# RWKV-7 recurrence in four products a chunk instead of five, its preparation in two threads instead of one

## The chip, the core and the metric

One core of a Trainium2 chip runs the whole program in one launch. Times are device microseconds (us) of that core. TensorE (PE) does matrix products and loads their weights through a queue of its own (PEld); VectorE (DVE) and ScalarE (ACT) do element work; GpSimd (POOL) does more of it; SyncE (SP) issues the DMAs. Each engine runs its own instructions in the order in which they stand, and waits on semaphores for the others.

## The reference

One inference step of a streaming encoder, one layer, on 512 prompt frames and 32 sample frames (544 columns). An input projection feeds three branches: Mamba-2 (SSD), gated linear attention (GLA) and RWKV-7. Gated output projections, cross attention over 256 memory tokens and a final norm follow. The change lies in the RWKV-7 branch, 16 heads of 64:

```
def step(S, inp):
    r_t, w_t, k_t, v_t, kk_t, a_t = inp
    s_kk = jnp.einsum('bhvk,bhk->bhv', S, kk_t)
    S_new = (S * w_t[:, :, None, :] - s_kk[..., None] * (kk_t * a_t)[:, :, None, :]
             + v_t[..., None] * k_t[:, :, None, :]).astype(S.dtype)
    return S_new, jnp.einsum('bhvk,bhk->bhv', S_new, r_t)
```

The output also has a bonus, the sum over a head of r, k and a weight, times v.

## The kernel before

**Layout.** Features lie on the 128 partitions, the 544 frames along the free axis. A weight block is 128 by 1024; it is loaded (`wraw`), split into a high part (`wh`, ACT) and a low part (`wl`, DVE), and multiplied in 24 products of 272 columns for each half of the frames: the "dense" products, `pd`. There are 7584 of them, and 56 blocks (`fill`) are not needed early; their results go through two `fg` buffers on ACT to DRAM.

**The order.** A planner (`Sched`) writes one static order for each engine. Each piece of work is a generator (a thread) with a priority; when a thread waits for data the next one gets a turn, and `dense` (priority 9) puts five `pd` products at a time into TensorE's queue. The planner estimates each instruction's time (`Sched.mm` for products) and uses only these estimates to choose the order. DMAs are queued on SP when the planner thinks that their data are there.

**RWKV in the planner.** Heads are taken in pairs (p = 0 to 7), one head on partitions 0 to 63, one on 64 to 127, frames in nine chunks of 64 (eight of the prompt and one, padded, of the sample). For each pair: `rw_A` prepares (shift, decay `EE`, keys, the operands `ar` and `bk`), then makes the pairwise products `pp` within chunks, masks them into `NK`, stores the matrices to be inverted (`n_scr`), computes the bonus (`pbn`), and turns v and the scaled keys into token rows (`ptk`, `tm`, twelve `NK<-tm` DMAs and four `NK<-t`). It does all of it for pair p before it begins pair p + 1. `rw_I` inverts the 32 by 32 diagonal blocks on POOL in 62 instructions (`im`, `td`) after the DMAs `nd` and `td<-in_eye`; `rw_J` brings the result back through DRAM (`d_scr`, `TT`), transposes it on DVE, and makes the last block with products `pW` and `pT`. `rw_C` is the recurrence: `pr` for all chunks, then for each chunk one after the other the products `pc`. `rw_N` normalises and writes out. Pairs use three slots of buffers.

In a chunk with a state `Sn` (128 partitions by 64: head 0 above head 1) before, the five products are two with the state, one with the inverse `TT`, and two with `NK`:

```
S.mm(pa[:, 0:64], AR[:, c, 0:2, :].rearrange("p a t -> p (a t)"), Ss, True, True)
S.mm(px, AR[:, c, 2:4, :].rearrange("p a t -> p (a t)"), Ss, True, True)
S.tt(R, pa[:, 0:64], NK[:, c, 0, 0, :], ADD)
S.mm(pu, TTt[:, c, :], R, True, True)
nc.vector.copy_predicated(VU, two(C("blk1").bitcast(I32)), both(pu))
    S.mm(pb[:, i * 64:i * 64 + 64], NK[:, c, i, 1:3, :].rearrange("p a t -> p (a t)"), VU[:, i, :], True, True)
```

All of these are full fp32 products, and the trace has two records for each. The recurrence has 72 chunks: 64 have a state before them, and the first prompt chunk of each of the eight pairs has none (one product with `TT` and two with `NK`).

Of the kernel before, what the change touches and what calls it, by code (L numbers as in the profile page):

```python
# [20 lines left out]
T = NP_ + NS  # L21
# [48 lines left out]
for _n, _c in (("ident", 128), ("blk1", 128), ("m_rw", 128), ("s65", 585), ("m_ssd", 128), ("s64", TP), ("s128", T)):  # L70
    CC.add(_n, _c)


def constants():
    c = np.zeros((128, CC.n), np.float32)

    def put(name, a):
        o, n = CC.at[name]
        c[:, o:o + n] = a

    p = np.arange(128)
    same = (p[:, None] // 64 == p[None, :] // 64).astype(np.float32)
    put("ident", np.eye(128))
    put("blk1", same)
    s = (p % 64)[:, None]
    t = np.arange(64)[None, :]
    put("m_rw", np.concatenate([s < t, s <= t], 1))
# [38 lines left out]
class Sched:  # L126
# [110 lines left out]
    def mm(self, out, lhsT, rhs, start, stop, transpose=False, shared=False):  # L237
# [102 lines left out]
def body(tc, I, O):  # L340
# [19 lines left out]
    with tc.manual_schedule(), \  # L360
# [418 lines left out]
        def make_slot(pool, i):  # L779

            d = dict(AR=pool.tile([128, 9, 4, 64], F32, name=f"AR{i}"))
# [10 lines left out]
        for i in range(2):  # L792
            nc.gpsimd.memset(f32(w2l[64 - 64 * i:128 - 64 * i, i]), 0.0)
        b_scr = dr.tile([8, 128, T], F32, name="b_scr")
# [83 lines left out]
        def rw_A(p):  # L878

            rs, ks, vs = (zt[p % 2][n_] for n_ in ("rs", "ks", "vs"))  # L880
            yield has("wa_s")
# [3 lines left out]
            if p < NSLOT:  # L885

                for h in (0, 64):
                    g = 64 - h
                    for x in (d["AR"][h:h + 64, :, 1:3, :] if h == 0 else d["AR"][h:h + 64, :, 0:4:3, :], d["TT"][h:h + 64, :, g:g + 64]):
                        nc.gpsimd.memset(x, 0.0)  # L890
                        S.note("p", 700, (x,), ())
# [29 lines left out]
            rn = rwp.tile([128, TP], F32, name="rn", tag="rn")  # L921
# [54 lines left out]
            for i in range(2):  # L976
                hs = slice(64 * i, 64 * i + 64)
                S.tt(ar[hs, :, 3 - i, :], ch(rs)[hs], EE[hs, :, 1:65], MUL)
# [18 lines left out]
            def tokens(n_, src):  # L997
# [8 lines left out]
                for i in range(2):  # L1006
                    h = 64 * i
                    g = h if n_ == 2 else 64 - h
                    for r in range(2):
                        S.store(out=nk[g:g + 64, r:8:2, i, 1 + i if n_ else 3, :], in_=tm[r * 64:r * 64 + 64, :, h:h + 64])  # L1010
# [5 lines left out]
            for c0, cn in ((0, 4), (4, 4), (8, 1)):  # L1016
# [3 lines left out]
                for c in range(cn):  # L1020
                    for i in range(2):
                        hs = slice(64 * i, 64 * i + 64)
                        S.mm(ps[i][:, c * 128:c * 128 + 128], bk[hs, c0 + c, i:i + 2, :].rearrange("p a t -> p (a t)"),
                             ar[hs, c0 + c, i:4 - i:3 - 2 * i], True, True)
                for i in range(2):
                    S.tt(nk[:, c0:c0 + cn, i, 0:3 - i:2 - i, :], ps[i][:, :cn * 128].rearrange("p (c a t) -> p c a t", c=cn, a=2),
                         two(C("m_rw")).unsqueeze(1).to_broadcast([128, cn, 2, 64]), MUL)
                yield S.free("v")
            for i in range(2):
                S.store(out=rows64(n_scr[p % 2], i), in_=nk[i * 64:i * 64 + 64, :, i, 0, :])  # L1030
            done.add(f"rwN{p}")

            r2 = rwp.tile([128, 3, TP], F32R, name="r2", tag="bk")
# [18 lines left out]
            for i in range(2):  # L1052
                h = 64 * i
                S.store(out=nk[64 - h:128 - h, 8, i, 1 + i:4:2 - i, :], in_=t8[:, 0:2, h:h + 64])
                S.store(out=nk[h:h + 64, 8, i, 1 + i, :], in_=t8[:, 2, h:h + 64])
# [37 lines left out]
        def rw_J(p):  # L1093
# [33 lines left out]

        def both(a):
# [3 lines left out]
        def rw_C(p):  # L1132
# [3 lines left out]
            s0r = rwp.tile([128, 64], F32, name="s0r", tag="s0r")  # L1136
            S.dma(out=s0r, in_=I["s0_rwkv"][:, p])
# [4 lines left out]
            yield S.at(s0r, NK, TTt)  # L1142
            for c0, cn in ((4, 5), (0, 4)):
                ps = yield from bank("pr")
                for c in range(cn):
                    for i in range(2):
                        hs, gs = slice(64 * i, 64 * i + 64), slice(64 - 64 * i, 128 - 64 * i)
                        S.mm(ps[hs, c * 64:c * 64 + 64], NK[gs, c0 + c, i, 0, :], NK[gs, c0 + c, i, 3, :], True, True)
                S.act(NK[:, c0:c0 + cn, 0, 0, :], ps[:, :cn * 64].rearrange("p (c t) -> p c t", t=64), AF.Copy)
            for c in [8] + list(range(8)):  # L1150
                Ss = s0r if c == 8 else (None if c == 0 else st_)
# [4 lines left out]
                pu, px = pa[:, 64:128], pb[:, 128:192]  # L1156
                VU, R = NK[:, c, :, 3, :], NK[:, c, 0, 0, :]
# [5 lines left out]
                yield S.at(R)  # L1163
                S.mm(pu, TTt[:, c, :], R, True, True)
                nc.vector.copy_predicated(VU, two(C("blk1").bitcast(I32)), both(pu))
                S.note("v", 203, (VU,), (pu,))
                yield S.at(VU)
                for i in range(2):
                    S.mm(pb[:, i * 64:i * 64 + 64], NK[:, c, i, 1:3, :].rearrange("p a t -> p (a t)"), VU[:, i, :], True, True)
                ns = rwp.tile([128, 64], F32, name="Sn", tag="S", bufs=2)  # L1170
                for i in range(2):
                    hs = slice(64 * i, 64 * i + 64)
                    if Ss is None:
                        S.cp(ns[hs], pb[hs, hs])
                    else:
                        S.stt(ns[hs], Ss[hs], GC[hs, c, :], pb[hs, hs], MUL, ADD)
                if c >= 7:
                    S.store(out=O["rwkv_s" if c == 8 else "rwkv_p"][:, p], in_=ns)
                st_ = ns
                yield S.at(ns)  # L1180
                for i in range(2):
                    gs = slice(64 - 64 * i, 128 - 64 * i)
                    S.act(NK[gs, c, 0, 3, :], pb[gs, i * 64:i * 64 + 64], AF.Copy)
                if Ss is not None:
                    S.act(NK[:, c, 1, 3, :], px, AF.Copy)
            done.add(f"rwC{p}")

        def rw_N(p):
# [4 lines left out]
            x = NK[:, :, 0, 3, :]  # L1193
            yield S.at(x)
# [7 lines left out]
            S.tt(x[:, 1:9], x[:, 1:9], NK[:, 1:9, 1, 3, :], ADD)  # L1202
            yield S.free("v")
            cs = rwr.tile([128, 9, 64], F32, name="cs", tag="cs")
            sq = rwr.tile([128, 9, 64], F32, name="sq2", tag="hi")
            S.stt(cs, sums("mean", x).to_broadcast([128, 9, 64]), -1.0 / 64, x, MUL, ADD)
# [753 lines left out]
        S.add(rw_all(rw_N, "rwN_end"), 2)  # L1960
        S.add(rw_all(rw_A), 3)
# [134 lines left out]
```

## Time and profile before

| what | value |
| --- | --- |
| median of 3 runs | 1306.12 us (1303.98 to 1306.37) |
| the profiled execution | 1309.07 us, of which its span 1307.3 us |
| PE busy | 1270.0 us, 97% of the span |
| DVE, ACT, POOL busy | 825.6, 637.2, 387.3 us |
| stretch with the recurrence | 165 to 665 us of the span |

The profile is of one execution. Its own time is 2.95 us above the median and 1.8 us above its span. Busy time of PE is from the start of a record to its modelled end, and records overlap, so the price of a product is read here from the distance between starts. A wait in the middle of a busy stretch shows only where it is longer than that overlap.

### The profile page before, as it was taken

How to read it: one execution, taken by the hardware profiler on the slowest of the kernel's cores; microseconds unless marked ns; L12 is line 12 of the kernel's file. 1: busy time of each engine (PE TensorE's matmuls, PEld its weight loads, DVE VectorE, ACT ScalarE, POOL GpSimd, SP SyncE). 2: the span in 40 equal slices, each digit the busy share in tenths (PEclk: the TensorE clock that was granted, in tenths of full speed). 3: DMA queues.
4: the chain of work that ended last, by engine and by line, in shares of the span. 5: the costliest groups of instructions: out<-in, count | busy, mean ns of one | idle time of the engine just before them, and what ended most of it. 6: DMA issues, size and time to landing. Idle time of an engine off the chain costs nothing.

```text
span 1307.3 us, 27775 instructions
## 1 busy us (share of the span) xinstructions
PE 1270.0 (97%) x10976; PEld 1226.2 (94%) x10976; DVE 825.6 (63%) x1643; ACT 637.2 (49%) x1263; POOL 387.3 (30%) x716
## 2 busy tenths in 40 slices
PE   8899998999999999999999999999999999999997
PEld 7899988999999999999999999988899999999997
DVE  5748646766766676754346687886666756575543
ACT  5664525375655555553455545463445423544422
POOL 0711747482827272833001062422300000000000
PEclk9999998999999999999999999998999999999999
DMA  8543544535353625364343243343698446540302
GB/s 290 161 140 92 148 100 130 132 118 134 121 127 111 153 90 148 122 161 134 109 168 122 91 127 109 115 132 104 231 337 288 140 136 189 170 146 25 105 17 70
DMA packets 170003, 181.10 MB, mean 139 GB/s; under 512 B 100096, under 2 KB 122720, under 8 KB 169744
## 3 DMA queue, kind: packets, MB, share of 16 engines
q1 hardware_dynamic: 169440, 178.64, 44.8%
q8 instruction: 87, 1.43, 0.5%
q10 hardware_dynamic: 432, 0.67, 0.2%
q14 instruction: 44, 0.36, 0.1%
HBM read 136.24 MB, written 35.39 MB: 131 GB/s over the span
## 4 chain that ended last, share of the span: by engine, by line
PE 81%; DVE 7%; ACT 3%; DMA 3%; POOL 3%; issue 2%; SPq 1%; POOLq 0%; ACTq 0%; DVEq 0%
PE pd L245 62%; PE pc L245 5%; PE pp L245 1%; DMA wraw<-in_wall 1%; DVE wl L284 1%; PE psc L245 1%; SPq L327 1%; PE pov L245 1%; PE pO L245 1%; PE py L245 1%; PE ptk L242 1%; DVE ul L293 1%; POOL im L284 1%; PE pl L245 1%; PE ph L245 1%
## 5 line engine op out<-in xcount | busy, mean ns | idle before, releaser
L245 PE MATMUL pd<-ul,wh 128*128 128x272 f32 (+1 forms) x1632 | 436.0, 295 | 0.0
L245 PE MATMUL pd<-uh,wh 128*128 128x272 f32 (+1 forms) x1632 | 432.5, 295 | 0.5 <-ACT wh L278 0.4
L245 PEld LDWEIGHTS pd<-ul,wh 128*128 128x128 f32 (+1 forms) x1632 | 309.1, 189 | 4.1 <-issue 2.4
L245 PEld LDWEIGHTS pd<-uh,wh 128*128 128x128 f32 (+1 forms) x1632 | 308.5, 189 | 4.0 <-ACT wh L278 1.6
L245 PE MATMUL pd<-uh,wl 128*128 128x272 f32 (+1 forms) x1632 | 252.5, 293 | 1.3 <-DVE wl L284 1.3
L245 PEld LDWEIGHTS pd<-uh,wl 128*128 128x128 f32 (+1 forms) x1632 | 221.1, 189 | 4.6 <-issue 1.9
L284 DVE TENSOR_TENSOR wl<-wraw,wh 128x1024 fp32r<-128x1024 f32 (+1 forms) x143 | 180.2, 1263 | 22.7 <-ACT wh L278 22.2
L278 ACT ACTIVATE wh<-wraw 128x1024 fp32r<-128x1024 f32 (+1 forms) x143 | 149.3, 1046 | 55.0 <-PE pd L245 36.4
L284 POOL TENSOR_TENSOR im<-td,nd 108x84 f32<-108x84 f32 (+23 forms) x248 | 106.0, 428 | 195.3 <-DMA td<-in_eye 86.2
L245 PE MATMUL pd<-uh,wr 128*128 128x256 f32 (+1 forms) x768 | 148.6, 291 | 1.4 <-ACT uh L278 1.4
L245 PEld LDWEIGHTS pd<-uh,wr 128*128 128x128 f32 x768 | 121.0, 188 | 3.0 <-ACT uh L278 1.6
L284 POOL TENSOR_TENSOR td<-td,im 108x84 f32<-108x84 f32 (+23 forms) x248 | 111.5, 450 | 19.4
L284 POOL TENSOR_TENSOR macc<-macc,hrs 128x288 f32<-128x288 f32 x3 | 2.3, 792 | 367.9 <-DVE macc L293 367.9
L245 PE MATMUL pd<-ul,wr 128*128 128x256 f32 (+1 forms) x384 | 100.2, 292 | 0.1
L245 PEld LDWEIGHTS pd<-ul,wr 128*128 128x128 f32 x384 | 72.4, 189 | 1.0 <-issue 0.4
L278 ACT ACT_TABLE_LOAD x55 | 70.6, 1283 | 2.6 <-DVE tB L284 1.6
L278 ACT ACTIVATE fg<-pd 128x272 f32<-128x272 f32 x64 | 25.1, 394 | 84.0 <-PE pd L245 62.6
L293 DVE SCALAR_TENSOR_TENSOR fg<-fg,pd 128x272 f32<-128x272 f32 x48 | 20.8, 435 | 61.6 <-ACT fg L278 61.4
L278 ACT ACTIVATE lerpA<-pd,par 128x272 f32<-128x272 f32 x50 | 24.3, 487 | 65.8 <-PE pd L245 61.1
L278 ACT ACTIVATE NK<-pc 64x64 f32<-64x64 f32 (+1 forms) x208 | 38.3, 214 | 34.2 <-DVE Sn L293 31.0
L278 ACT ACTIVATE fg<-pd,dpar 128x272 f32<-128x272 f32 x48 | 23.1, 484 | 61.1 <-PE pd L245 48.6
L293 DVE SCALAR_TENSOR_TENSOR Sn<-Sn,GC,pc 64x64 f32<-64x64 f32 x112 | 31.2, 279 | 25.7 <-PE pc L245 22.0
(470 smaller groups left out, 2479.5 us busy)
## 6 DMA issues: line engine op xcount, KB each, us to landing
wraw<-in_wall SPq DMA_DIRECT2D x165, 512.0 KB
g_mg<-fg SPq DMA_DIRECT2D x24, 272.0 KB
mgt<-g_mg SPq DMA_DIRECT2D x24, 272.0 KB
NK<-tm SPq DMA_DIRECT2D x96, 64.0 KB
ab<-acs_d SPq DMA_DIRECT2D x8, 512.0 KB
nd<-n_scr SPq DMA_DIRECT2D x24, 144.0 KB
n_scr<-NK SPq DMA_DIRECT2D x16, 144.0 KB
TT<-d_scr SPq DMA_DIRECT2D x16, 144.0 KB
```

The costliest lines, as they stand in the source:

```text
L242: self.nc.tensor.transpose(out, lhsT, rhs)
L245: self.nc.tensor.matmul(out, lhsT, rhs, start=start, stop=stop, skip_group_check=shared)
L278: self.nc.scalar.activation(out=out, in_=in_, func=f, scale=scale, bias=bias)
L284: eng.tensor_tensor(out=out, in0=a, in1=b, op=op)
L293: self.nc.vector.scalar_tensor_tensor(out=out, in0=a, scalar=s, in1=b, op0=op0, op1=op1)
L327: getattr(self.nc, q).dma_start(out=out, in_=in_)
```

## The change

**In `rw_C`** the state is held as a 128 by 128 block-diagonal tile `Sb` (three of them, zeroed once), so one product of 128 moving columns replaces the two with the state, and the product with `TT` gets 128 columns too. `R` is twice as wide. The three evacuations on ACT become two of 128 by 128. The state's load and its two stores become two DMAs of half the size each. For a chunk without a state POOL zeroes the place of the missing part (8 new instructions). `AR` halves, so 6 memsets of it go from POOL. **In `rw_N`** one addition over 128 partitions becomes two over 64. **The planner's estimate** for an fp32 product of over 64 rows out changes. **`rw_A` is cut** after the keys; the new thread `rw_B` has the rest. `rw_A(p+1)` may begin when `rw_A(p)` has ended; it waits for the bonus of pair p before it reuses `r2`, for the masked products before it reuses `bk`, and for `rwA{p-2}`.

```
-                ns = max(107.0, n * 1.67)
+                ns = max(220.0, n * 1.79)
...
+        Sb = [rwp.tile([128, 2, 64], F32, name=f"Sb{i}") for i in range(3)]
...
-            yield has("wa_s")
+            yield has("wa_s", *([f"rwA{p - 2}"] if p > 1 else []))
...
-            sq = rwp.tile([128, TP], F32, name="sq", tag="sq")
+            sq = rwp.tile([128, TP], F32, name="sq", tag="sq", bufs=2)
...
-            k2 = rwp.tile([128, 3, TP], F32R, name="k2", tag="bk")
+            if p:
+                yield has(f"rwB{p - 1}")
+            k2 = rwp.tile([128, 2, TP], F32R, name="k2", tag="r2")
...
+            if p:
+                yield has(f"rwN{p - 1}")
             bk = rwp.tile([128, 9, 3, 64], F32, name="bk", tag="bk")
...
+            hand[p] = rs, vs, kae, bee, bk, d
             done.add(f"rwK{p}")
-            yield has("rwR", f"vs{p}")
+        def rw_B(p):
+            yield has(f"rwK{p}", "rwR", f"vs{p}")
+            rk, vs, kae, bee, bk, d = hand.pop(p)
...
                 if Ss is not None:
-                    S.mm(pa[:, 0:64], AR[:, c, 0:2, :].rearrange("p a t -> p (a t)"), Ss, True, True)
-                    S.mm(px, AR[:, c, 2:4, :].rearrange("p a t -> p (a t)"), Ss, True, True)
-                    R = rwp.tile([128, 64], F32, name="R", tag="R")
-                    S.tt(R, pa[:, 0:64], NK[:, c, 0, 0, :], ADD)
+                    S.mm(pa[:, 0:128], AR[:, c].rearrange("p a t -> p (a t)"), Ss, True, True)
+                    r_ = rwp.tile([128, 2, 64], F32, name="R", tag="R")
+                    S.tt(r_, two(pa[:, 0:128]), R, ADD)
+                    R = r_
...
-                for i in range(2):
-                    gs = slice(64 - 64 * i, 128 - 64 * i)
-                    S.act(NK[gs, c, 0, 3, :], pb[gs, i * 64:i * 64 + 64], AF.Copy)
+                S.act(NB[:, c, 3:8:4, :], two(pb[:, 0:128]), AF.Copy)
                 if Ss is not None:
-                    S.act(NK[:, c, 1, 3, :], px, AF.Copy)
+                    S.act(NB[:, c, 0:7:6, :], two(pa[:, 0:128]), AF.Copy)
+                else:
+                    nc.gpsimd.memset(NB[:, c, 0:7:6, :], 0.0)
...
+        S.add(rw_all(rw_B), 3)
         S.add(rw_all(rw_A), 3)
```

Three places of the order show what moves. On TensorE, one step of the recurrence of pair 0, before:

```order
L245 MATMUL pc<-Sn,AR_119 128x64 x2
L245 MATMUL pd<-ul,wh 128x272
L245 MATMUL pd<-uh,wh 128x272
L245 MATMUL pd<-ul,wh 128x272
L245 MATMUL pd<-uh,wh 128x272
L245 MATMUL pd<-ul,wh 128x272
L245 MATMUL pc<-R,TT_121 128x64
L245 MATMUL pbn<-r_3026,blk_97 128x272 x4
L242 MATMUL ptk<-con,rn 128x128 x4
L245 MATMUL pc<-NK_120 128x64 x2
```

and the step of the same pair that stands first in the order of the change (`Sb` is the state, `R` the sum that goes into the product with `TT`):

```order
L245 MATMUL pc<-Sb_133,AR_119 128x128
L245 MATMUL pd<-ul,wh 128x272
L245 MATMUL pd<-uh,wl 128x272 x4
L245 MATMUL pc<-R,TT_121 128x128
L245 MATMUL pd<-uh,wl 128x272 x4
L245 MATMUL pd<-uh,wh 128x272
L245 MATMUL pd<-ul,wh 128x272
L245 MATMUL pd<-uh,wh 128x272
L245 MATMUL pd<-ul,wh 128x272
L245 MATMUL pd<-uh,wh 128x272
L245 MATMUL pc<-NK_120 128x64 x2
```

The two products of 128x64 with the state have become one of 128x128, the one with `TT` is 128x128, the two with `NK` are as they were, and five dense products stand between state and `TT` in both.

On ScalarE, the last rows before the evacuation of `pr` with which the recurrence of pair 0 begins, before:

```order
L278 ACTIVATE fg<-pd 128x272 x2
L278 ACTIVATE wh<-wraw 128x1024
L278 ACTIVATE W<-pW 128x256
L278 ACTIVATE TT_121<-pT 32x8x32 x2
L278 ACTIVATE fg<-pd 128x272
L278 ACTIVATE NK_120<-pr 128x5x64
L278 ACTIVATE NK_120<-pr 128x4x64
```

and now:

```order
L278 ACTIVATE fg<-pd 128x272
L278 ACTIVATE wh<-wraw 128x1024
L278 ACTIVATE lerpA<-pd,par 128x272
L278 ACTIVATE W<-pW 128x256
L278 ACTIVATE lerpA<-pd,par 128x272
L278 ACTIVATE wh<-wraw 128x1024
L278 ACTIVATE TT_121<-pT 32x8x32 x2
L278 ACTIVATE NK_120<-pr 128x5x64
L278 ACTIVATE NK_120<-pr 128x4x64
```

Of three `fg` evacuations ahead of `NK<-pr` one is left; `lerpA` (the token shift of later pairs) stands there instead.

On SP, from the store of the matrices of pair 1 (`n_scr`) to the load of its unit matrices (`td<-in_eye`), with which its inversion can begin; `d_scr` and `TT` belong to pair 0. Before:

```order
L327 DMA n_scr_135<-NK_124 64x9x64 x2
L327 DMA nd<-n_scr_135 36x32x32 x3
L327 DMA b_scr<-rs_109 128x544
L327 DMA NK_124<-tm 64x4x64 x8
L327 DMA td<-in_eye 108x352
L327 DMA g_rwkv<-fg 128x544
L327 DMA wraw<-in_wall 128x1024
```

and now:

```order
L327 DMA n_scr_141<-NK_124 64x9x64 x2
L327 DMA w2r<-in_w2a 128x256
L327 DMA b_scr<-rs_109 128x544
L327 DMA NK_124<-tm 64x4x64 x8
L327 DMA d_scr<-td 36x11x32
L327 DMA d_scr<-td 36x10x32
L327 DMA d_scr<-td 36x11x32
L327 DMA TT_121<-d_scr 64x9x64 x2
L327 DMA nd<-n_scr_141 36x32x32 x3
L327 DMA wraw<-in_wall 128x1024
L327 DMA td<-in_eye 108x352
```

The result of pair 0 (`d_scr`, `TT`) stood ahead of this piece; now it stands inside it, so the inversion of pair 1 follows directly on that of pair 0. Between the products `pW` of pair 0 and those of pair 1 TensorE has 312 dense products and 40 products `pc` before, 211 and 27 now; between pair 1 and pair 2 it has 297 and 39 before, 240 and 31 now. In all, TensorE's order has 64 products fewer; every other kind of product keeps its count.

## Rows read from the trace of the kernel before

**Rows 1.** The page: span, busy time of each engine, chain that ended last.

```profile
span 1307.3 us, 27775 instructions
PE 1270.0 (97%) x10976; PEld 1226.2 (94%) x10976; DVE 825.6 (63%) x1643; ACT 637.2 (49%) x1263; POOL 387.3 (30%) x716
PE 81%; DVE 7%; ACT 3%; DMA 3%; POOL 3%; issue 2%; SPq 1%; POOLq 0%; ACTq 0%; DVEq 0%
```

**Rows 2.** Windows, 165 to 665 us: length, busy us of each engine, clock, DMA share.

```profile
165.00:665.00 500.00, 489.59 (x4758) 475.06 (x4759) 305.98 (x667) 255.94 (x584) 239.93 (x517) 0.99 0.46 125
```

**Rows 3.** Waits of TensorE: us in total, times, longest.

```profile
PE pc L245 <- DVE R L284: 4.7, 2, 4.4
```

**Rows 4.** Timeline of a recurrence step of pair 7: start us, us, instruction.

```profile
653.35 0.65 PE L245 MATMUL pd<-uh,wl 128*128 128x272 f32 x4
653.84 0.55 PE L245 MATMUL pc<-Sn,AR 128*128 128x64 f32 x4
654.20 0.75 PE L245 MATMUL pd<-uh,wl 128*128 128x272 f32 x4
654.21 0.23 DVE L284 TENSOR_TENSOR R<-pc,NK 128x64 f32<-128x64 f32 x1 [0.89 <-PE pc L245]
654.79 0.33 PE L245 MATMUL pc<-R,TT 128*128 128x64 f32 x2
```

**Rows 5.** Timeline of fp32 products with 128 moving columns (GLA stage).

```profile
740.43 0.38 PE L245 MATMUL pO<-AT,vt 128*128 128x128 f32 x2
740.65 0.39 PE L245 MATMUL pO<-g_qe,gS 128*128 128x128 f32 x2
```

**Rows 6.** Tile `pc`: products with the state, ns min/median/max, first and last start.

```profile
L245 PE MATMUL pc<-Sn,AR x224: 217/275/323, 213.0 to 657.6; 128*128 128x64 f32 x112
L245 PE MATMUL pc<-s0r,AR x32: 275/275/323, 190.9 to 628.1; 128*128 128x64 f32 x32
```

**Rows 7.** Groups by form on DVE and ACT: count, busy us, mean ns, idle before.

```profile
L284 DVE TENSOR_TENSOR R<-pc,NK 128x64 f32<-128x64 f32 x64 | 14.2, 222 | 30.0 <-PE pc L245 20.9 <-ACT NK L278 5.2 <-PE pd L245 3.1
L284 DVE TENSOR_TENSOR NK<-pp,con 128x128 f32<-128x128 f32 x16 | 3.9, 285 | 0.7 <-PE pp L245 0.5
L278 ACT ACTIVATE NK<-pc 64x64 f32<-64x64 f32 x144 | 31.3, 218 | 34.2 <-DVE Sn L293 31.0 <-DVE Sn L305 1.2
L278 ACT ACTIVATE btok<-pcb 128x128 f32<-128x128 f32 x8 | 1.9, 264 | 4.0 <-PE pcb L245 3.9
```

**Rows 8.** Timeline, 185 to 201 us, of PE, SP and ACT.

```profile
185.85 0.83 PE L245 MATMUL pW<-x,NK 32*64 32x32 f32 x22
...
189.38 6.14 SPq L327 DMA_DIRECT2D NK<-tm  x8
...
196.24 0.35 SPq L327 DMA_DIRECT2D g_rwkv<-fg  x1
...
199.16 0.40 ACT L278 ACTIVATE fg<-pd 128x272 f32<-128x272 f32 x1 [9.94 <-DMA g_rwkv<-fg]
```

**Rows 9.** Windows right after that wait; columns as in rows 2.

```profile
200.20:206.20 6.00, 5.98 (x27) 5.98 (x28) 2.56 (x7) 3.58 (x7) 3.76 (x11) 0.51 0.72 262
```

**Rows 10.** Timeline of the inversion of pair 1 and the start of pair 2's.

```profile
198.54 0.24 POOL L284 TENSOR_TENSOR im<-td,nd 108x31 f32<-108x31 f32 x1 [19.75 <-DMA td<-in_eye]
...
239.94 1.28 SPq L327 DMA_DIRECT2D d_scr<-td  x3
...
244.01 1.28 SPq L327 DMA_DIRECT2D TT<-d_scr  x2
...
250.15 2.12 SPq L327 DMA_DIRECT2D nd<-n_scr  x3
...
252.16 1.12 PE L245 MATMUL pW<-x,NK 32*64 32x32 f32 x32
252.31 1.00 SPq L327 DMA_DIRECT2D td<-in_eye  x1
...
256.99 0.24 POOL L284 TENSOR_TENSOR im<-td,nd 108x31 f32<-108x31 f32 x1 [17.08 <-DMA td<-in_eye]
```

More of the change, by code (lines that the diff above doesn't have):

```diff
@@ L69 @@
 CC = Cols()
-for _n, _c in (("ident", 128), ("blk1", 128), ("m_rw", 128), ("s65", 585), ("m_ssd", 128), ("s64", TP), ("s128", T)):
+for _n, _c in (("ident", 128), ("blk1", 128), ("m_rw", 192), ("s65", 585), ("m_ssd", 128), ("s64", TP), ("s128", T)):
     CC.add(_n, _c)
@@ L86, in constants @@
     t = np.arange(64)[None, :]
-    put("m_rw", np.concatenate([s < t, s <= t], 1))
+    put("m_rw", np.concatenate([s < t, s <= t, s < t], 1))
     put("m_ssd", p[:, None] <= p[None, :])
@@ L793, in body @@
             nc.gpsimd.memset(f32(w2l[64 - 64 * i:128 - 64 * i, i]), 0.0)
+        Sb = [rwp.tile([128, 2, 64], F32, name=f"Sb{i}") for i in range(3)]
+        for t_ in Sb:
+            nc.gpsimd.memset(t_, 0.0)
         b_scr = dr.tile([8, 128, T], F32, name="b_scr")
@@ L888, in rw_A @@
                     g = 64 - h
-                    for x in (d["AR"][h:h + 64, :, 1:3, :] if h == 0 else d["AR"][h:h + 64, :, 0:4:3, :], d["TT"][h:h + 64, :, g:g + 64]):
-                        nc.gpsimd.memset(x, 0.0)
-                        S.note("p", 700, (x,), ())
+                    x = d["TT"][h:h + 64, :, g:g + 64]
+                    nc.gpsimd.memset(x, 0.0)
+                    S.note("p", 700, (x,), ())
             w2h = rwp.tile([128, 2, 128], F32R, name="w2h", tag="w2h")
@@ L1009, in tokens @@
                     for r in range(2):
-                        S.store(out=nk[g:g + 64, r:8:2, i, 1 + i if n_ else 3, :], in_=tm[r * 64:r * 64 + 64, :, h:h + 64])
+                        S.store(out=nk[g:g + 64, r:8:2, i, 1 if n_ else 3, :], in_=tm[r * 64:r * 64 + 64, :, h:h + 64])
                 yield S.free("a")
@@ L1023, in rw_A @@
                         S.mm(ps[i][:, c * 128:c * 128 + 128], bk[hs, c0 + c, i:i + 2, :].rearrange("p a t -> p (a t)"),
-                             ar[hs, c0 + c, i:4 - i:3 - 2 * i], True, True)
+                             ar[hs, c0 + c], True, True)
                 for i in range(2):
-                    S.tt(nk[:, c0:c0 + cn, i, 0:3 - i:2 - i, :], ps[i][:, :cn * 128].rearrange("p (c a t) -> p c a t", c=cn, a=2),
-                         two(C("m_rw")).unsqueeze(1).to_broadcast([128, cn, 2, 64]), MUL)
+                    S.tt(nk[:, c0:c0 + cn, i, 0:3:2, :], ps[i][:, :cn * 128].rearrange("p (c a t) -> p c a t", c=cn, a=2),
+                         two(C("m_rw")[:, 64 * i:64 * i + 128]).unsqueeze(1).to_broadcast([128, cn, 2, 64]), MUL)
                 yield S.free("v")
             for i in range(2):
-                S.store(out=rows64(n_scr[p % 2], i), in_=nk[i * 64:i * 64 + 64, :, i, 0, :])
+                S.store(out=rows64(n_scr[p % 2], i), in_=nk[i * 64:i * 64 + 64, :, i, 2 * i, :])
             done.add(f"rwN{p}")
-            r2 = rwp.tile([128, 3, TP], F32R, name="r2", tag="bk")
+            r2 = rwp.tile([128, 2, TP], F32R, name="r2", tag="r2")
             rh, rl = r2[:, 0], r2[:, 1]
@@ L1053, in rw_A @@
                 h = 64 * i
-                S.store(out=nk[64 - h:128 - h, 8, i, 1 + i:4:2 - i, :], in_=t8[:, 0:2, h:h + 64])
-                S.store(out=nk[h:h + 64, 8, i, 1 + i, :], in_=t8[:, 2, h:h + 64])
+                S.store(out=nk[64 - h:128 - h, 8, i, 1:4:2, :], in_=t8[:, 0:2, h:h + 64])
+                S.store(out=nk[h:h + 64, 8, i, 1, :], in_=t8[:, 2, h:h + 64])
             done.add(f"rwA{p}")
@@ L1135, in rw_C @@
             yield has(f"rwA{p}")
-            s0r = rwp.tile([128, 64], F32, name="s0r", tag="s0r")
-            S.dma(out=s0r, in_=I["s0_rwkv"][:, p])
+            for i in range(2):
+                S.dma(out=Sb[2][64 * i:64 * i + 64, i], in_=I["s0_rwkv"][64 * i:64 * i + 64, p])
             yield has(f"rwI{p}")
@@ L1141, in rw_C @@
             yield S.stored(NK)
[L1142 removed]
+            yield S.at(Sb[2], NK, TTt)
             for c0, cn in ((4, 5), (0, 4)):
@@ L1200, in sums @@
                 return t
-            S.tt(x[:, 1:9], x[:, 1:9], NK[:, 1:9, 1, 3, :], ADD)
+            for i in range(2):
+                gs = slice(64 - 64 * i, 128 - 64 * i)
+                S.tt(cs[gs], NB[gs, :, 6 * i, :], NB[gs, :, 3 + 4 * i, :], ADD)
             yield S.free("v")
-            cs = rwr.tile([128, 9, 64], F32, name="cs", tag="cs")
-            sq = rwr.tile([128, 9, 64], F32, name="sq2", tag="hi")
-            S.stt(cs, sums("mean", x).to_broadcast([128, 9, 64]), -1.0 / 64, x, MUL, ADD)
+            S.stt(cs, sums("mean", cs).to_broadcast([128, 9, 64]), -1.0 / 64, cs, MUL, ADD)
             done.add(f"rwO{p}")
```

44 lines of the change are left out of this document (26 added, 18 removed).

## The prediction

> **What bounds the kernel now.** First the busy shares and the chain that ended last [rows 1]: TensorE is busy for 97% of the span, and 81% of the chain is its own work. So the time is TensorE's work plus its waits, and a shorter chain on another engine is worth only the wait that it removes. Second the windows: in the stretch with the recurrence TensorE is busy for 489.6 of 500 us, while DVE, ACT and POOL have 306, 256 and 240 us of work [rows 2]; nothing else is near its limit there. The recurrence is a long chain, but dense products stand between its steps. If the chain gets shorter, these dense products are done later, beside the SSD and GLA stages; they are not saved. Third the waits: the longest of TensorE in that stretch is 4.4 us of the 4.7 us on the sum `R` [rows 3].
>
> **The products that go.** A fp32 product has two records. The price is the delay that it makes for the dense products behind it. Before the step of pair 7 four dense products take 0.49 us from start to start (653.35 to 653.84). The two products with the state start at 653.84, the next dense product at 654.20, 0.36 us later, and its four take 0.59 us, 0.10 us too many. So the two cost 0.46 us, 0.23 us each [rows 4]. Products with 128 moving columns start 0.22 us apart [rows 5]. So a product costs the same at 64 columns and at 128, to 0.01 us, and making the two remaining ones twice as wide is free, while one of five goes. The state's products of before are (224 + 32) / 2 = 128 [rows 6]; 64 are left. I take the lower price: 64 x 0.22 = 14.1 us less (14.7 us by the higher one).
>
> The Trainium skill says otherwise: "TensorE: Matmul & The Clock Gate", section "Back-to-back issue gap", lets the distance of matmuls grow with the moved columns. The rows just cited speak against it for these fp32 products; what it would make of the time stands with the rivals.
>
> **What the wider step costs elsewhere.** `R` goes from 128x64, 222 ns, to 128x128, for which the masked products have the same operation, shape and operands (PSUM and SBUF): 285 ns [rows 7]. That is 63 ns more between the state product and the one with `TT`. On ACT two evacuations of 128x128 at 264 ns, as `btok` shows, take the place of three smaller ones of which two are 218 ns [rows 7]; about 0.1 us less per chunk, on an engine that has time to spare. The addition in `rw_N` is one more DVE instruction in a pair, and its readers wait in a thread of their own: hidden by dense work, and without that cover less than 1 us a pair (the 128x128 sum takes 0.29 us, a quarter of the columns and twice the rows). The 24 more DMAs on SP, at 0.35 us as the store in rows 8, are 8.4 us of a queue that serves 500 us; I cost them at nothing, and if they fall into one of SP's piles they are part of the bound for SP below. The eight memsets on POOL wait for the product of a chunk that TensorE has reached by then; behind them stands the inversion of the next pair, which is where their cost would show.
>
> In the shown step `R` starts 0.37 us after the state product, takes 0.23, and TensorE reads it at 654.79, 0.35 us after its end. Between state and `TT` stand four or five dense products, about 0.6 us, at some 20 places before and now. The first state product was followed by a second of 0.22 us, which was cover; it is gone. At the tight places 0.22 + 0.06 us of cover is lost against the 0.35 us that the row shows to spare, so many should still fit. Bounds: nothing, or 64 x 0.063 = 4.0 us when every longer `R` is waited for. I take 2 us.
>
> The cut between `rw_A` and `rw_B` adds no instruction: its waits hold back the planner's threads, not an engine, and what they do is seen in the order alone. It brings the keys and products of the next pairs forward, which is where the next two points come from.
>
> **A wait that should go.** Until 200.2 us TensorE stands for 4.4 us for the first `R` of pair 0 [rows 3]. The chain behind it is in rows 8: SP is busy with eight `NK<-tm` from 189.38 for 6.1 us, the store `g_rwkv` gets its turn at 196.24, ACT's next `fg` waited 9.9 us for that store (both buffers full), and behind `fg` on ACT stand the evacuations that `R` needs. Right after it TensorE's clock is at 0.51, the lower of its two levels (1.2 of 2.4 GHz), for 6.0 us [rows 9]; that costs another 6.0 x 0.49 = 2.9 us. In the new order only one `fg` stands near there, and none between `W` and `NK<-pr`. So this wait should go: 7.3 us less. SP's pile is still there, longer by `d_scr`, `TT` and `nd`, so the same can happen to a weight load; then the gain is 0.
>
> **A wait that should come.** The inversions of the pairs now follow each other directly. One cycle, from one `TT` to the next, by rows 10: `TT` 1.3, `nd` 2.1, one weight load 0.4, `td` 1.0, from its end to the first POOL instruction 3.7, the 62 instructions 41.4 (198.54 to 239.94), then 4.1 from `d_scr` to `TT`, of which 2.6 us went to four `NK<-tm` ahead of it. (The weight load is put at about the 0.35 us of the store in rows 8.) That is 54 us at most. In pair 1 the order of before has eight other POOL instructions among the 62 (memsets, decays, keys), the new one two; 41.4 us over 70 is 0.6 us each, so some 3.5 us go, 38 stay, and without the `NK<-tm` the cycle is 48 us. So: 48 to 54. TensorE's own work between `pW` of pair 0 and of pair 1: before 252.16 - 185.85 = 66.3 us [rows 8, 10], less the 7.3 us above, 59.0; 101 dense products fewer at 0.123 and 13 `pc` fewer at 0.22 make it 43.7 us. Between pairs 1 and 2 it is about 47 us by the same counts. What is missing is 4 to 10 us at pair 1 and 1 to 7 at pair 2, less what lay between the landing of `TT` and `pW` (8.2 us from issue to `pW` in pair 1, of which the way through DRAM and the transposes need a part, perhaps half). From pair 3 on 269 to 293 dense products stand between, with room. I take 3 us at each of the two: 6 us. Bounds: 0, and 13 us.
>
> **The sum.** 1309.07 - 14.1 - 7.3 + 2 + 6 = 1295.7 us for an execution like the profiled one. That one was 2.95 us above the median of its three runs, so the median to expect is 1292.7: **1293 us**.
>
> **The rivals.**
>
> *The new waits give little or nothing back.* The inversion keeps up, and the longer `R` is hidden. 1306.1 - 14.1 - 7.3 = 1285 us. For it: POOL has half its time free in the stretch [rows 2]. Against: its work is one chain with DMAs at both ends.
>
> *The inversion becomes the pace (slower).* Place: `pW` of each pair, for `TT`. With 54 us a cycle pairs 1 and 2 miss 10 and 7 us, less 4: 13 us; two waits of such length would each bring a stretch at the lower clock as in rows 9, 5.8 us; with R's 2 us, -14.1 - 7.3 + 13 + 5.8 + 2 leaves 1305.5, no change. Some 53 to 55 us a cycle is the point that decides. At 58 us pairs 1, 2 and 4 miss 14, 11 and 6, less 4: 27 us and three slow stretches, 8.7: 1306.1 - 21.4 + 27 + 8.7 + 2 = 1322 us. For it: POOL's 41.4 us are of a stretch with fewer instructions on DVE per us. Against: six instructions fewer stand there in pair 1.
>
> *A wait is only moved.* The products go, but SP's pile holds up a weight load or an `fg` elsewhere at the old price: 1306.1 - 14.1 + 2 + 6 = 1300 us.
>
> *The columns set the price.* If a wide product cost 0.22 and a narrow one half of it, a chunk would cost 5 x 0.11 = 0.55 before and 2 x 0.22 + 2 x 0.11 = 0.66 now; 64 x 0.11 = 7 us more, 1313 us. This is the rule named above. Against it stands 0.23 against 0.22 in rows 4 and 5.
>
> *The change doesn't do what it says:* the order shows the 64 products gone, so only their price is open.
>
> **How the numbers follow.** Forecast as summed, 1288 to 1299: 0.50. Nothing given back, below 1288: 0.17. A wait only moved, 1299 to 1303.5: 0.12. Inversion near its deciding point, no change: 0.08; slower: 0.10. Columns: 0.03, slower. A measurement of this kernel tells apart about 0.2%, 2.6 us. So faster 0.79, same 0.08, slower 0.13. The range leaves a few in a hundred below (both gains and small waits of TensorE gone too) and the inversion's bad end above: 1282 to 1306.
>
> **What would show it.** Tile `pc` with 128 records for the state instead of 256, starts of a wide product still 0.22 us apart; no `fg` wait of 9.9 us; in TensorE's waits `pW` (through the DVE transpose or ACT) with a few us at pairs 1 and 2; POOL's 62 instructions of pair 1 in about 38 us. The prediction is wrong if TensorE's idle time in the stretch grows by over 14 us, or if the wide product costs more than 0.3 us.

## The result, and the profile after

The changed kernel takes **1316.84 us** (median of 4 runs, 1313.06 to 1320.48), the kernel before 1305.43 us in the same session: a ratio of 1.008 [1.006, 1.0099], slower by 0.8%. The forecast was 1293 us, range 1282 to 1306, with 0.13 for slower: outside the range, and of the wrong sign.

The page of the changed kernel: span, busy times, and the chain that ended last.

```profile
span 1318.6 us, 27544 instructions
PE 1270.8 (96%) x10848; PEld 1222.5 (93%) x10848; DVE 838.5 (64%) x1651; ACT 626.8 (48%) x1191; POOL 380.3 (29%) x721
PE 66%; DVE 8%; ACT 4%; POOL 3%; DMA 3%; issue 3%; SPq 0%; POOLq 0%; ACTq 0%; DVEq 0%
```

The 128 instructions of TensorE are gone (10848 instead of 10976), but the chain has changed [rows 1]: 81% of it was TensorE's work, now it is 66%. The windows show where, columns as in [rows 2].

```profile
165.00:665.00 500.00, 475.49 (x4522) 456.12 (x4521) 313.28 (x667) 246.58 (x511) 242.59 (x524) 0.97 0.45 123
...
470.60:477.40 6.80, 5.64 (x26) 5.57 (x26) 4.56 (x12) 1.88 (x4) 0.00 (x0) 0.50 0.72 134
235.00:242.00 7.00, 6.81 (x57) 6.53 (x58) 1.70 (x7) 1.68 (x5) 5.94 (x16) 0.51 0.43 156
532.00:539.00 7.00, 6.67 (x30) 6.11 (x30) 3.52 (x11) 1.64 (x4) 0.00 (x0) 0.51 0.74 187
```

In the stretch with the recurrence TensorE is busy for 475.5 of 500 us, 14.1 less than before [rows 2]: it waits more (the prediction named over 14 us of idle time as a sign that it is wrong). Behind three of its long waits (5.76 us until 471.76, 1.95 until 235.19, 2.69 until 532.26) its granted clock is at 0.50 and 0.51, the lower of its two levels. The waits themselves:

```profile
PE pc L245 <- DVE R L284: 9.1, 6, 5.8
PE pc L245 <- DVE Sb L293: 6.1, 5, 2.7
PE pp L245 <- POOL bk L305: 3.2, 1, 3.2
PE pc L245 <- DVE NK L1185: 3.0, 3, 2.4
```

`R` alone was 4.7 us [rows 3]; `R`, `Sb` and `NK` are the three results of DVE in a recurrence step, 18.2 us now. The timeline around the longest wait says why (rows of POOL, SP, PE and DVE, from the inversion to the product that waited):

```profile
460.10 0.22 POOL L284 TENSOR_TENSOR td<-td,im 108x11 f32<-108x11 f32 x1
460.34 1.90 SPq L327 DMA_DIRECT2D d_scr<-td  x3
...
462.35 2.68 SPq L327 DMA_DIRECT2D NK<-tm  x4
...
464.49 0.38 PE L245 MATMUL pc<-Sb,AR 128*128 128x128 f32 x2
...
465.13 0.55 SPq L327 DMA_DIRECT2D wraw<-in_wall  x1
...
465.79 1.28 SPq L327 DMA_DIRECT2D TT<-d_scr  x2
...
470.19 0.44 DVE L1120 STREAM_TRANSPOSE x<-TT 64x256 f32<-64x256 f32 x1 [5.68 <-DMA TT<-d_scr]
470.94 0.44 DVE L1120 STREAM_TRANSPOSE x<-TT 64x256 f32<-64x256 f32 x1 [0.32 <-DMA TT<-d_scr]
471.42 0.29 DVE L284 TENSOR_TENSOR R<-pc,NK 128x128 f32<-128x128 f32 x1
...
471.76 0.80 PE L245 MATMUL pc<-R,TT 128*128 128x128 f32 x2 [5.76 <-DVE R L284]
...
474.40 0.95 PE L245 MATMUL pc<-NK 128*128 128x64 f32 x4
```

The inversion of the next pair ends on POOL at 460.3. SP issues its stores, then four `NK<-tm` and a weight load that stand ahead, then the load of `TT`. DVE's queue has come to the transposes of that `TT` and waits 5.68 us for it. Behind them in the same queue stands `R` of the recurrence under way, whose products ended long before, and TensorE waits for `R`. The wait until 532.26 has the same cause; ahead of the one until 235.19 DVE's queue was held for `wh` (2.16 us) instead, and so for a weight load. Over the kernel DVE is idle for 13.1 us ahead of the 16 transposes. The first line is of the kernel before, with 1.4 us:

```profile
L1104 DVE STREAM_TRANSPOSE x<-TT 64x256 f32<-64x256 f32 x16 | 7.0, 437 | 1.4 <-DMA TT<-d_scr 1.2
...
L1120 DVE STREAM_TRANSPOSE x<-TT 64x256 f32<-64x256 f32 x16 | 7.0, 438 | 13.1 <-DMA TT<-d_scr 13.0
L284 DVE TENSOR_TENSOR R<-pc,NK 128x128 f32<-128x128 f32 x64 | 18.4, 288 | 36.0 <-PE pc L245 28.7 <-ACT NK L278 6.9
```

### The profile page after: what moved, and what is told of

It reads as the page before. It is cut to its first block, busy times and chain, and to the rows that moved or that the text cites. A ratio compares the mean times of both kernels' runs of the same rounds, so it can differ in the third digit from the quotient of the medians.

```text
span 1318.6 us, 27544 instructions
## 1 busy us (share of the span) xinstructions
PE 1270.8 (96%) x10848; PEld 1222.5 (93%) x10848; DVE 838.5 (64%) x1651; ACT 626.8 (48%) x1191; POOL 380.3 (29%) x721
## 4 chain that ended last, share of the span: by engine, by line
PE 66%; DVE 8%; ACT 4%; POOL 3%; DMA 3%; issue 3%; SPq 0%; POOLq 0%; ACTq 0%; DVEq 0%
PE pd L245 50%; PE pc L245 4%; PE psc L245 1%; PE pO L245 1%; PE py L245 1%; POOL td L284 1%; DVE wl L284 1%; PE pov L245 1%; DMA wraw<-in_wall 1%; POOL im L284 1%; ACT L278 1%; DMA TT<-d_scr 1%; PE pp L245 1%; PE ph L245 1%; DVE cs L284 1%
## 5 line engine op out<-in xcount | busy, mean ns | idle before, releaser
L284 POOL TENSOR_TENSOR im<-td,nd 108x84 f32<-108x84 f32 (+23 forms) x248 | 114.1, 460 | 110.3 <-DMA td<-in_eye 53.3
L293 DVE SCALAR_TENSOR_TENSOR Sb<-Sb,GC,pc 64x64 f32<-64x64 f32 x128 | 35.6, 279 | 30.9 <-PE pc L245 28.7
L278 ACT ACTIVATE NK<-pc 128x128 f32<-128x128 f32 x136 | 30.4, 274 | 41.4 <-DVE Sb L293 34.2
L245 PE MATMUL pc<-NK 128*128 128x64 f32 x288 | 44.8, 280 | 3.3 <-DVE NK L1185 3.0
L245 PEld LDWEIGHTS pc<-NK 128*128 128x128 f32 x288 | 39.5, 197 | 7.0 <-DVE NK L1185 4.5
```

Of the source, the lines that this page charges most:

```text
L278: self.nc.scalar.activation(out=out, in_=in_, func=f, scale=scale, bias=bias)
L284: eng.tensor_tensor(out=out, in0=a, in1=b, op=op)
L293: self.nc.vector.scalar_tensor_tensor(out=out, in0=a, scalar=s, in1=b, op0=op0, op1=op1)
```

## The experiments

The change has three parts: the four products of a step, the two threads, and one line that the prediction had not priced, the planner's estimate of a fp32 product (from `max(107, 1.67 n)` to `max(220, 1.79 n)` ns). Three theories stood at first. A: the threads let the inversions follow each other directly, and DVE's queue is held for `TT`, as just shown. B: the new estimate takes slack out of the order. C: the four-product step itself makes TensorE wait. Two came up on the way. D: the removed products only covered waits. O: the order of before is a tuned one, and an order drawn anew is worse. Brackets are 95% intervals; where two ratios are subtracted, the ± is worked out from theirs. The kernel before was measured again beside each group of runs, and the ratios go to those runs of it.

| run | us, median | ratio to before |
|---|---|---|
| e1 products | 1305.28 | 1.0004 [0.9986, 1.0022] |
| e2 products, estimate | 1314.28 | 1.0077 [1.0053, 1.01] |
| e3 products, threads | 1311.49 | 1.0056 [1.0034, 1.0078] |
| e4 whole change, late transposes | 1305.94 | 1.0013 [0.9996, 1.003] |
| e5 products, late transposes | 1307.75 | 1.0023 [1.0011, 1.0035] |
| e6 before, late transposes | 1320.72 | 1.0133 [1.0113, 1.0153] |
| e7 products, state product doubled | 1312.3 | 1.0063 [1.0048, 1.0079] |
| e8 products, more margin | 1337.15 | 1.025 [1.0225, 1.0274] |
| e9 before, one product less | 1300.66 | 0.996 [0.994, 0.998] |
| e10 whole change, no hold | 1311.68 | 1.0037 [1.0025, 1.0049] |
| e11 before, estimate | 1324.16 | 1.0139 [1.0122, 1.0157] |
| e12 products, threads, late | 1301.04 | 0.9964 [0.9951, 0.9978] |
| e13 before, estimate 5% up | 1310.86 | 1.0041 [1.0025, 1.0057] |
| e14 before, estimate 5% down | 1313.88 | 1.0071 [1.0055, 1.0087] |
| e15 products, threads, no hold | 1303.12 | 0.999 [0.9976, 1.0004] |
| e16 products, threads, 4 us late | 1311.02 | 1.0052 [1.0032, 1.0072] |

**The parts alone.** e1 is the changed kernel with one preparation thread and the old estimate; e2 has the new estimate with it, e3 the two threads:

```diff
 e1, e3 against the changed kernel
-                ns = max(220.0, n * 1.79)
+                ns = max(107.0, n * 1.67)
 e1, e2 against the changed kernel
-        S.add(rw_all(rw_B), 3)
...
+            yield has("rwR", f"vs{p}")
```

> Four products alone: one thread for the preparation and the old estimate of an fp32 product. Theory A (the cut into two threads lets the inversions follow each other directly; the transposes of TT then hold VectorE's queue for a DMA, and the recurrence's own sums stand behind them): no direct succession, so VectorE is idle under 3 us before x<-TT, and the products' 14 us show: 1290 to 1297 us. Theory B (the new estimate takes slack out of the order): also 1290 to 1297. Theory C (the four-product step itself, with the wider R and one product less of cover, makes TensorE wait): 1303 to 1316, with waits of pc on R, Sb and NK as in the changed kernel (18 us).

> Four products and the new estimate (220 ns at least), still one thread. Theory A: as with the products alone, 1290 to 1298 us, VectorE idle under 3 us before x<-TT. Theory B: 1308 to 1318 us, close to the changed kernel, with pc waits of 15 us and more. Theory C: 1303 to 1316.

> Four products and two threads, with the old estimate. Theory A: 1308 to 1318 us, VectorE idle about 10 us before x<-TT and pc waits of 10 us and more. Theory B: 1290 to 1298 us, since the old estimate leaves the engines beside TensorE some 5 us more per pair than the order counts on. Theory C: 1303 to 1316.

The products alone are worth nothing. C was right in this time, but not in its waits: those of `pc` on `R`, `Sb` and `NK` are 7.3 us in e1, not 18. The estimate on top of them costs 0.73%, 9.5 us, the time that B forecast, but without B's waits of 15 us and more: they are 7.5 us in e2. The threads on top of the products cost 0.52%, 6.8 us; e3 has the 8.6 us of idle DVE and the 11.6 us of waits that A expected. With both the change stands at 1.008, so the two don't add up.

**The transposes later.** e4 is the whole change; e5, e6 and e12 have the same edit in other kernels, e16 with 4000.

```diff
-            yield S.at(tt_)
+            yield S.at(tt_) + 6000.0
```

> The whole change, with the DVE transposes of TT put into the order 6 us later (the planner's thread waits that much longer after it thinks that TT has landed). No wait is taken away, only the place in VectorE's queue. Theory A: the 13 us that VectorE stands before x<-TT fall to under 3, the long waits of pc (5.8, 2.7, 2.4 us) and the stretches of low clock behind them go: 1298 to 1305 us. Theory B or C: these waits have other causes and stay: 1312 to 1320 us.

> The four-product step alone (one preparation thread, old estimate), with the DVE transposes of TT placed 6 us later in the order. Where the transposes stood at the head of DVE's queue, DVE was idle for 4.3 us before them with the products alone, 13.1 with the whole change. Theory A (the held DVE queue is what takes the gain): 1300 to 1303, 2 to 5 us below the products alone (1305.3), and below before. Theory D (the 14 us come back as small waits of the recurrence itself, because its step has lost its cover): 1304 to 1307, no difference to the products alone.

> The kernel before, with the DVE transposes placed 6 us later, a control. DVE is idle for only 1.4 us before them there. Theories A and D both: 1304 to 1307, no difference to before. If it gains as much as in the whole change (11 us), the place of the transposes is worth something whatever the change is, and the fourth run says nothing about the change.

> Products and two threads with the old estimate, and the DVE transposes placed 6 us later. Theory A (two threads make the inversions follow each other, and the hold on DVE's queue for TT is their price): 1301 to 1306, 6 to 10 us below the same without the late placing (1311.5). If the place of the transposes helps only by chance of the order, as the late placing in the kernel before (1320.7) suggests: anything from 1306 to 1320.

> Products and two threads, old estimate, transposes placed 4 us later instead of 6 (which gave 1301.0). Theory A: 1300 to 1304, since 4 us cover most of the holds (longest 5.7 us in the change). Theory O: 1303 to 1315, as 1301.0 was one lucky order.

In e4 DVE's idle time ahead of the transposes falls from 13.1 to 0.4 us and the change loses its loss, about as A expected. But e5 gains nothing from the same edit though its hold went from 4.3 to 0.3 us, e6 loses 17 us, and of e12 and e16, which differ in 2 us of placing, one is the fastest kernel of this study that computes the whole result and the other is slower than before. The edit draws the whole order anew, and that weighs more than the hold. In e6 the new waits are in other places (waits of TensorE):

```profile
PE pd L245 <- ACT wh L278: 6.4, 4, 2.6
PE py L245 <- DVE seg L284: 6.1, 1, 6.1
PE pd L245 <- DVE fg L293: 3.5, 1, 3.5
```

**The same order without the hold.** e10 is the whole change, e15 the same in e3. Only the operand of the transposes differs, so the blocks under the diagonal of the inverse are left out; the order of the instructions is the same on every engine.

```diff
-                nc.vector.transpose(x1[h:h + 64], tt_[h:h + 64, 0:8, h:h + 32])
+                nc.vector.transpose(x1[h:h + 64], con[h:h + 64, 0:256].rearrange("p (c j) -> p c j", c=8))
```

> The whole change in its own order, but the DVE transposes read a constant tile instead of TT (the blocks under the diagonal come out wrong), so that DVE's queue isn't held for the DMA of TT. Nothing else moves on any engine. Theory A (the held queue is what costs): 1301 to 1307, 10 to 15 us below the change's 1316.8, since 13.1 us of DVE idle go and most of the waits on R, Sb and NK with their low clock. Theory B and C (order and cover): at most 4 us below, 1313 or more.

> Products and two threads with the old estimate (1311.5), same order on every engine, but the DVE transposes read a constant tile and so don't wait for TT (blocks under the diagonal come out wrong). Theory A (the threads' price is the hold on DVE, idle 8.6 us before these transposes): 1304 to 1308. If it is the order otherwise (small waits, low clock): 1309 to 1312.

The same step as in the timeline above, in e10:

```profile
458.82 0.88 DVE L1120 STREAM_TRANSPOSE x<-con 64x256 f32<-64x256 f32 x2
458.89 0.38 PE L245 MATMUL pc<-Sb,AR 128*128 128x128 f32 x2
...
459.73 0.29 DVE L284 TENSOR_TENSOR R<-pc,NK 128x128 f32<-128x128 f32 x1
...
460.24 0.39 PE L245 MATMUL pc<-R,TT 128*128 128x128 f32 x2
...
461.60 0.55 PE L245 MATMUL pc<-NK 128*128 128x64 f32 x4
```

From the state product to the one with `TT` it is 1.35 us instead of 7.27. Between the two profiled executions the recurrence is 13.6 us shorter (last `pc` product at 623.5 instead of 637.1), but by the ratios of all runs the hold is worth 0.43% ± 0.23, 5.6 us, less than A's 10 to 15. The profiled execution of e10 (1306.8 us) is the fastest of its twelve, that of the changed kernel (1320.5) the slowest of its four. In e3 the hold is worth 0.66% ± 0.26, 8.6 us by the ratios, as much as the threads cost. The traces of e3 and e15 don't show that gain: the two profiled executions took 1306.7 and 1306.9 us, the fastest but one of the twelve of e3 and the slowest but one of the twelve of e15. In e15 the waits on `Sb` fell from 9.7 to 0.3 us, and those on `R` rose from 1.1 to 4.8.

**The product itself.** e7 issues the state product twice, e9 leaves the second state product of the kernel before out, and with it that part of the output; each keeps the order of the kernel that it is made from. e8 asks for 0.3 us more of dense products at each hand-over of a step.

```diff
 e7, against e1
+                    nc.tensor.matmul(pa[:, 0:128], AR[:, c].rearrange("p a t -> p (a t)"), Ss, start=True, stop=True)
 e9, against before (not issued, but booked by the planner)
-                    S.mm(px, AR[:, c, 2:4, :].rearrange("p a t -> p (a t)"), Ss, True, True)
...
-                    S.act(NK[:, c, 1, 3, :], px, AF.Copy)
+                    S.act(NK[:, c, 1, 3, :], px, AF.Copy, src=pa[:, 0:64])
 e8, against e1 (and the same at R and ns)
-                yield S.at(VU)
+                yield S.at(VU) + 300.0
```

> The four-product step alone, in the same order, with the product of the state issued twice (64 more products of 128x128 by 128 columns, same result), right behind the first one. It puts back the work and the cover that the removed product had. If a removed product is worth its 0.22 us where it stands: 1317 to 1320, 12 to 14 us above the products alone. Theory D (TensorE waits in these places anyway, so the removed product only uncovered a wait): 1305 to 1310, at most 5 us above.

> The kernel before with nothing else changed than that the second product with the state is not issued (its place in the planner's books is kept, so the order on every engine stays the same; ACT copies the first product's columns in its place, so part of the result is left out). 64 products fewer, narrow R. If a removed product is worth 0.22 us where it stands: 1290 to 1292, 13 to 15 us below before. Theory D (it only covered a wait, as the doubled product suggested for half of it): 1297 to 1305.

> The four-product step alone, with 0.3 us more of dense products asked for at each of the three hand-overs of a recurrence step (before the TT product, before the two NK products, before the next state product). Theory D: the small waits on R, NK and Sb (7.3 us in the profile of the products alone) go, and with them the stretches at the lower clock that they start in some executions: 1297 to 1302. If the 14 us are lost anywhere else: 1304 to 1308; if the longer steps push the recurrence past its stage: above 1310.

The groups of `pc` by form in e9 (count, busy us, mean ns, idle ahead), then the same of before:

```profile
L245 PE MATMUL pc<-NK 128*128 128x64 f32 x288 | 41.7, 268 | 1.3 <-DVE lerpA L802 0.8 <-issue 0.3
L245 PE MATMUL pc<-R,TT 128*128 128x64 f32 x128 | 23.3, 264 | 7.7 <-DVE R L284 7.2 <-DVE lerpA L802 0.3
L245 PE MATMUL pc<-Sn,AR 128*128 128x64 f32 x112 | 19.3, 254 | 1.1 <-DVE Sn L293 1.1
L245 PE MATMUL pc<-s0r,AR 128*128 128x64 f32 x16 | 3.5, 300 | 2.2 <-DMA s0r<-in_s_rwkv 2.2
```

```profile
L245 PE MATMUL pc<-NK 128*128 128x64 f32 x288 | 40.9, 264 | 0.6 <-DVE lerpA L802 0.5
L245 PE MATMUL pc<-Sn,AR 128*128 128x64 f32 x224 | 31.7, 264 | 0.4 <-DVE Sn L293 0.4
L245 PE MATMUL pc<-R,TT 128*128 128x64 f32 x128 | 22.4, 257 | 4.9 <-DVE R L284 4.7
L245 PE MATMUL pc<-s0r,AR 128*128 128x64 f32 x32 | 5.2, 286 | 0.4 <-DMA s0r<-in_s_rwkv 0.4
```

Idle time ahead of these products goes from 6.3 to 12.3 us: 6.0 of the 14.1 us come back as waits. Since the order is the same, the two traces can be laid on each other product by product. From state product to `TT` product the median step is 0.22 us shorter, as priced, and 52 of the 64 are shorter by more than 0.15; the 64 sum to 10.6 us, since a few steps wait for something that the removed work doesn't set.

The dearest is the first of pair 4 (from 455.06 before, 449.07 in e9): there `R` needs the `NK` that ACT copies from `pr` at 452.82, which the removed product doesn't make earlier, the step goes from 3.0 to 4.5 us, and TensorE stands for 1.7. A further 4.4 us are given back between a step's `NK` products and the next state product, less 1.2 us gained between `TT` and `NK` products. From the first `pc` product (190.9; e9: 191.3) to the last (660.1; 653.3) 7.2 us are left; by the ratio it is 0.4% [0.2, 0.6], 5.2 us.

In e7 the doubled product makes the median step 0.22 us longer and the kernel 0.59% ± 0.24, 7.7 us. It is not the removal turned round: `R` reads what both copies write and starts 0.64 us after the state product at the earliest (0.42 in e1), while in the kernel before it reads the first product alone (0.37). So e7 puts the work back, but not the cover. In e9 D holds for 8.9 of the 14.1 us, though not step by step. More margin (e8) is no remedy: the waits on `NK` and `Sb` fall from 5.9 us to 1.4, but those on `R` rise from 1.4 to 6.7, `wh`, `gw` and `seg` take over 5 us each in the stages behind, and the mean granted clock is 0.976.

**The estimate, and the order as such.** e11 is the new line in the kernel before, e13 and e14 are small steps of it.

```diff
-                ns = max(107.0, n * 1.67)
+                ns = max(220.0, n * 1.79)
 e13
+                ns = max(112.0, n * 1.75)
 e14
+                ns = max(102.0, n * 1.59)
```

> The kernel before with the new estimate alone (220 ns instead of 107 for a product of 64 columns, 1.79 ns a column). Theory B (the estimate itself makes the order worse): 1311 to 1316, as on top of the products. If it only met the other parts badly: 1303 to 1308.

> The kernel before with the planner's estimate of a fp32 product 5% higher (112 ns and 1.75 a column), nothing else. No instruction is added or removed; only the order is drawn anew. Theory O (the order of before is a tuned one, and any re-drawn order loses some us to waits): 1309 to 1320. Theory E (the size of the estimate costs, 17 us for 113 ns): at most 2 us above before, 1304 to 1308.

> The same with the estimate 5% lower (102 ns and 1.59 a column). Theory O: 1309 to 1320. Theory E: 1303 to 1307, no loss, since a lower estimate only asks for more dense products between the steps.

In e11 the groups of `pc` read:

```profile
L245 PE MATMUL pc<-NK 128*128 128x64 f32 x288 | 42.3, 270 | 6.2 <-DVE NK L1165 5.7 <-DVE lerpA L802 0.5
L245 PE MATMUL pc<-Sn,AR 128*128 128x64 f32 x224 | 32.2, 266 | 4.8 <-DVE Sn L293 3.3 <-DVE lerpA L802 1.1
L245 PE MATMUL pc<-R,TT 128*128 128x64 f32 x128 | 24.2, 271 | 3.1 <-DVE R L284 3.0
```

Idle time there is 14.7 us with `s0r`'s 0.6, against 6.3. A planner that thinks a product longer believes that TensorE will be later, and asks for fewer dense products in between: the steps with at most five products between state and `TT` product go from 22 to 33 of 64. So the mechanism of B is there, for 8.4 of its 18 us. But e13 and e14 cost 5 and 9 us with an estimate moved by 5% either way, which the size of the estimate (theory E of these texts) can't explain. All four orders drawn from the kernel before without a change of its work (e6, e11, e13, e14) are slower than it, by 5 to 18 us. That fits O; that the order of before was tuned is not shown, nor that any other order is worse (in e12 below a new one, with fewer products, is faster).

Nor is the loss always where the edit was made. In the stretch with the recurrence e6, e13 and e14 are no worse than before (TensorE busy for 490.6, 491.6 and 491.7 of 500 us, 489.6 in [rows 2]); they lose behind it (from 665 to 1100 us TensorE is busy for 418.6, 425.9 and 421.4 of 435 us, before 430.6). The windows of e13 and e14, columns as in [rows 2], and two waits of e14: the one on `R` the kernel before has too [rows 3], the one on `seg`, at 919.5 us, is 1.4 us there.

```profile
165.00:665.00 500.00, 491.58 (x4769) 476.52 (x4769) 307.90 (x664) 255.41 (x580) 243.74 (x517) 0.99 0.46 125
...
165.00:665.00 500.00, 491.69 (x4783) 478.07 (x4784) 309.29 (x667) 258.45 (x585) 246.80 (x515) 0.99 0.45 125
```

```profile
PE py L245 <- DVE seg L284: 5.1, 1, 5.1
PE pc L245 <- DVE R L284: 4.0, 1, 4.0
```

**A version that beats both.** e12 (four products, two threads, old estimate, transposes 6 us later) has 1301.04 us, 0.36% below before and 1.2% below the changed kernel. Its waits on `R` are still 5.7 us; in the long window TensorE is busy as long as before, at clock 1.00, with less work to do:

```profile
165.00:665.00 500.00, 489.52 (x4722) 471.17 (x4721) 321.02 (x675) 251.73 (x521) 242.05 (x523) 1.00 0.47 128
```

Since e16 stands beside it at 1311, it is a good draw of the order and no proof that 6 us are right.

## Why the prediction was wrong, by its own steps

**The products that go (-14.1 us).** The price was right: in the changed kernel a wide product still takes 0.22 us from the dense products behind it. In the rows below the state product starts at 622.66, the dense product behind it at 622.80, the next one at 623.01. Together the two take 0.35 us; a dense product alone takes 0.13 (622.53 to 622.66), which leaves 0.22.

```profile
622.53 0.29 PE L245 MATMUL pd<-uh,wh 128*128 128x272 f32 x1
622.66 0.38 PE L245 MATMUL pc<-Sb,AR 128*128 128x128 f32 x2
622.80 0.37 PE L245 MATMUL pd<-ul,wh 128*128 128x272 f32 x1
623.01 1.17 PE L245 MATMUL pd<-uh,wl 128*128 128x272 f32 x8
```

The rival by which columns set the price is refuted: a narrow product is worth 0.22 us in the median step of e9, a wide one 0.22 in that of e7. What failed is the step from price to time, "a shorter chain on another engine is worth only the wait that it removes", which should have been asked of TensorE's own work too. The time comes from TensorE's work plus its waits; less work left the things that it waits for where they were, and in e9 5.2 [2.6, 7.8] of the 14.1 us were left.

The Trainium skill, "Perfetto Trace Analysis", section "Identifying the Most-Contended Engine", says to optimize the engine with the highest occupancy first, and to judge TensorE by the weight loads' busy share and by the share of its peak rate. The weight loads' share is 94% here [rows 1], so by the page TensorE is the engine to work on. How much of the removed work comes back as time the page doesn't say; here it was 5.2 of 14.1 us (e9).

**The longer `R` (+2 us).** It is 288 ns in the mean, 285 were expected. In e1 the wait for it is 1.4 us at six products, within the bounds.

**The wait that should go (-7.3 us).** Most of it went: at 194.09 TensorE waits 1.21 us for the first `R` of pair 0 where it waited 4.4, no `fg` there waits for its store, and the window behind it has clock 1.00:

```profile
194.09 0.49 PE L245 MATMUL pc<-R,TT 128*128 128x128 f32 x2 [1.21 <-DVE R L284]
```

```profile
194.00:200.00 6.00, 5.91 (x54) 5.62 (x55) 5.49 (x14) 2.50 (x6) 5.20 (x10) 1.00 0.30 96
```

**The wait that should come (+6 us, at `pW` of pairs 1 and 2).** The cause was named, the place was not. The inversions do follow each other (those of pairs 1 and 2 start 46.9 us apart), and the POOL work of pair 1 takes even less than the 38 us of the forecast, 187.2 to 219.3. But no product `pW` waits, so it is not the rival of the inversion as the pace either, between whose two times the result lies: what stops is DVE at the transposes ahead of `pW`, and the price is paid by the recurrence of the pair before, whose sums stand behind them in DVE's queue; the longest such wait stands at 471.76, long after pair 2, where the prediction saw room. By e10 it is worth 5.6 us, by e3 and e15 8.6; that this lies near the 6 us of the sum is luck, as those were counted at another wait.

**What the sum left out.** It read the new order at three places and put the rest at nothing. It had no term for the estimate, which stands in the diff, nor one for an order that is drawn anew for 1300 us. Drawing it anew without any change of work cost 5 to 18 us in all four tries. Of the change's 10.4 us over before, -5.2 for the product and +5.6 for the hold are measured in a fixed order, each to some 3 us; the other 10 us are the difference, if the two add up, and fit that range. They stand although the wait above mostly went. How much of them belongs to the estimate, to the wider step or to chance stays open: every run that would separate them draws its own order. Threads alone, without the four products, weren't tried.

The two profiled executions show in what form the time came. TensorE is not busy for 47.8 us of the span instead of 37.3, and it is busy as long as before (1270.8 and 1270.0 us) with 14.1 us less to do. Its mean granted clock is 0.985 instead of 0.990, by an estimate from the two spans some 6.5 us of that; what makes up the other 8 stays open.

## What to carry to other kernels

In a kernel whose order a planner lays out, an edit is two edits: what it does, and a new order everywhere. Price the second by its own (here 5 to 18 us, in four tries of four) before a gain of 1% is believed, and try a part in a fixed order, where two traces can be laid on each other instruction by instruction. When a step waits for a DMA, look at what else stands in the queue of the engine that waits, since that is where the time is lost.

## What the runs showed of the hardware

Work taken from an engine that is busy for 97% of the span gave back 37% of itself (5.2 of 14.1 us, e9). And the wait of 5.76 us cost more than its length. In the 6.80 us from 470.60, which begin inside it, TensorE is busy for 5.64 us at a granted clock of 0.50, by estimate another 2.8 us. Laid on e10, where that stretch has clock 1.00, the time from the state product to the one with `TT` is 5.9 us longer (7.27 against 1.35), and from there to the products with `NK`, where TensorE waits for nothing, it is still 1.3 us longer (2.64 against 1.36).
